# Second mixer: who scales the wide attention rows, and how the values are turned

## The chip, the core and the metric

The kernel runs on one core of one Trainium2 chip. The metric is device time in microseconds (us); each figure without another name is the median of several executions. TensorE (PE) does the matrix products, VectorE (DVE) and ScalarE (ACT) the work on vectors, GpSimd (POOL) and SyncE (SP) issue most of the transfers.

## What is computed

Two layers over 512 tokens of width 1024, in float32. The change lies in the mixer of the second layer: a band attention with 12 heads of 64 columns, whose keys and values are projected from the output of the first layer, beside an attention over 256 memory tokens. Cut to what matters:

```python
ks_, vs_ = jnp.split(rmsnorm(x, kv_norm_g) @ w_kv, 2, axis=-1)      # shared keys and values
...
q, q_mem = jnp.split(h @ b_w_in, [B_WIDTH], axis=-1)
s = jnp.einsum('bqhd,bkhd->bhqk', qc, kc).astype(jnp.float32) * scale + bias
s = jnp.where(valid, s, -jnp.inf)                                   # own chunk and 8 chunks before
p = jax.nn.softmax(s, axis=-1).astype(vc.dtype)
out = jnp.einsum('bhqk,bkhd->bqhd', p, vc)
x = x + jnp.concatenate([mix_out, mem_out], axis=-1) @ w_out
```

## The kernel before

Activations lie transposed: 128 features on the partitions, 512 tokens along the row. Each float32 operand of a product is split in two float32r parts, the high one by a cast on ACT and the low one by a subtraction on DVE (`split`, lines 146 to 151, where the work shows as L147 and L148), and `mm3` (lines 201 to 205) makes three matmuls of each product: high by high, high by low, low by high.

The second mixer goes through six pairs of heads, j = 0 to 5. `project_pair(j)` (line 1477) projects one pair's values, keys and queries: three calls of `project` (line 207), each of 8 k-tiles, so 24 matmuls of 512 columns, with its own weight load of 512 KB on SP's queue (line 162) into one of three "wr" tiles. `times_row` multiplies the projection by the norm's row (L1480). The values come out with features on the partitions, but the product with the attention needs tokens there. So PE turns them: four 128x128 transposes into one PSUM bank (L1491), after the keys' projection and before the queries'. Then `split` makes high and low parts of the turned values out of PSUM, half of the tokens at a time (line 1496; in the profile under L147 and L148).

`band_attention(j)` (line 1501) takes the four tiles T of 128 query tokens in turn, two heads each. `softmax(T)`: the scores of n = 128(T+1) columns on PE (L622); on DVE the bias is added and the row minimum taken (L1518); ACT takes the exponential with its row sum (L1522); DVE takes the sum's reciprocal (L1523) and scales the row by it (L1524). `transposed(T)` turns the scaled rows on PE, 128 columns at a time (L1533), and splits them. At the end the values multiply them (L1554, L1555).

The tiles of the tag "t", 128x512, have eight buffers; the values before they are turned, the scaled rows and the queries before their split all live there. The values' parts lie in "fh" and "fl" (in "u" for the last pair).

Order of the work: `weave` (line 234) mixes an attention with the projections that come later, which serve as its filler: after each step of the attention, so many steps of the filler (one step is one k-tile, three matmuls) by a number written by hand for each pair. Outside of sections marked as manually scheduled, which this one is not, a planner takes this as the order of preference, lets each engine's instructions go when its own costs say that they are ready and a buffer is free, and so writes down one order for each engine and each transfer queue. On the chip every engine and queue keeps to its order, and waits at the head of it.

Of the kernel before, what the change touches and what calls it, by code (L numbers as in the profile page):

```python
# [9 lines left out]
F32 = mybir.dt.float32  # L10
F32R = mybir.dt.float32r
I32 = mybir.dt.int32
AF = mybir.ActivationFunctionType
ALU = mybir.AluOpType
AX = mybir.AxisListType

P = 128
D = 1024
S = 512
KT = D // P  # L20
TT = S // P
# [27 lines left out]
UNITS = {PLAIN + i: tuple((i, j) for j in range(*LOADS[i][2:])) for i in range(len(LOADS))}  # L49

H = S // 2
ORDERED = {mybir.EngineType.PE, mybir.EngineType.Activation, mybir.EngineType.DVE}


def f(ap):
    return ap.bitcast(F32)
# [3 lines left out]
def trunk(  # L60
# [18 lines left out]
    nc = tc.nc  # L79
    V, A, G = nc.vector, nc.scalar, nc.gpsimd  # L80
# [12 lines left out]
    dram = ctx.enter_context(tc.tile_pool(name="dram", bufs=1, space=bass.MemoryType.DRAM))  # L93

    def sb(tag, shape, dtype=F32):
        count[0] += 1
        return pool.tile(shape, dtype, tag=tag, name=f"{tag}{count[0]}", bufs=bufs[tag])

    def ps(tag):
        count[0] += 1  # L100
        return psum.tile([P, S], F32, tag=tag, name=f"p{tag}{count[0]}", bufs=pbufs[tag])
# [12 lines left out]
    ident = cpool.tile([P, P], F32, name="ident")  # L114
# [79 lines left out]
    def weights(*args):  # L194
        return parts(load(*args))
# [11 lines left out]
    def project(w, c0, act, tag="mm", parts=None):  # L207


        n = len(act)  # L210
        wh, wl = parts or weights(rows(w, c0, P), n, P)
        o = ps(tag)
        for k in range(n):
            mm3(o, wh[:, k, :], wl[:, k, :], act[k][0], act[k][1], k == 0, k == n - 1)
            yield
        return o
# [167 lines left out]
    for k in range(KT):  # L384
        if k % 2 == 0:
            src = mem[:, k * P : (k + 2) * P].rearrange("(m p) c -> p m c", p=P)
# [53 lines left out]
    norm = Norm()  # L440
# [168 lines left out]
    def head_keys(t):  # L609
        ks = [sb("u", [P, S], F32R) for _ in range(2)]  # L610
        for h, r in enumerate(HEADS):
            A.copy(ks[h][r, :], t[r, :])
            V.tensor_tensor(out=ks[h][HEADS[1 - h], :], in0=t[r, :], in1=f(ks[h])[r, :], op=ALU.subtract)
        return ks
# [32 lines left out]
    def queries(o, row):  # L647

        if row is None:
            return head_queries(o, HD**-0.5)  # L650
        q = sb("t", [P, S])
        V.scalar_tensor_tensor(q, o, HD**-0.5, row, op0=ALU.mult, op1=ALU.mult)
        return head_queries(q)
# [89 lines left out]
    class ChannelMixer:  # L743
# [54 lines left out]
        def block_sums(self):  # L798

            self.sums = []  # L800
            for k in range(KT // 2):
# [6 lines left out]
                for o, x, y in (  # L808
                    (ta[:, :H], b1[:, H:], b1[:, :H]),
                    (ta[:, H:], b2[:, H:], ta[:, :H]),  # L810
                    (tb[:, :H], b2[:, H:], b1[:, H:]),
                    (tb[:, H:], b2[:, :H], ta[:, H:]),
                ):
# [342 lines left out]
    act = acts  # L1156
# [39 lines left out]
    e, u, c, r = (cpool.tile([P, TT, AH], F32, name=f"gate{i}") for i in range(4))  # L1196
# [253 lines left out]
    norm2, kvact, act = Norm(), [], []  # L1450
# [10 lines left out]
    norm = norm2  # L1461
# [15 lines left out]
    def project_pair(j):  # L1477
        def times_row(o):
            t = sb("t", [P, S])
            V.tensor_tensor(out=t, in0=o, in1=norm.row, op=ALU.mult)  # L1480
            return t

        ov = yield from project(w_kv, AW + j * P, kvact)
        t = times_row(ov) if norm.row is not None else None
        o = yield from project(w_kv, j * P, kvact)
        if t is None:
            t = times_row(ov)
        k = head_keys(times_row(o))
        tp = ps("mm")
        for T in range(TT):  # L1490
            nc.tensor.transpose(tp[:, T * P : (T + 1) * P], t[:, T * P : (T + 1) * P], ident)  # L1491
        v = []
        for i in range(2):

            w = sb("u" if j == 5 else ("fh", "fl")[i], [P, S], F32R).rearrange("p (h c) -> p h c", h=4)
            split(w[:, :, :HD], w[:, :, HD:], tp[:, i * MEM : (i + 1) * MEM].rearrange("p (h c) -> p h c", h=4))
            v += [w[:, :2, :], w[:, 2:, :]]
        q = queries((yield from project(b_w_in, j * P, act)), norm.row)
        qkv[j] = q, k, v

    def band_attention(j, q, k, v):
        pts = [sb("pt", [P, 5 * S], F32R) for _ in range(2)]
        biases = []
        for h in range(2):
            rep = reps[2 * j + h]
            biases.append(sb("bias", [P, S]))
            src = bass.AP(tensor=rep.tensor, offset=rep.offset + P - 1, ap=[[RW - 1, P], [1, S]])
            tc.keep_in_program_order(G.dma_start(biases[h], src))
        es = {}

        def softmax(T):
            n = (T + 1) * P
            ss = [ps("sc")[:, :n] for _ in range(2)]
            scores(ss, q, slice(T * P, n), k, slice(0, n))
            for h in range(2):
                e = sb("t", [P, S])[:, :n]
                mn, sm = small(1), small(1)
                V.tensor_tensor_reduce(  # L1518
                    out=e, in0=ss[h], in1=biases[h][:, S - n :], scale=-1.0, scalar=BIG,
                    op0=ALU.add, op1=ALU.min, accum_out=mn,  # L1520
                )
                A.activation(e, e, AF.Exp, bias=mn, scale=-1.0, accum_out=sm)  # L1522
                V.reciprocal(sm, sm)  # L1523
                V.tensor_scalar(e, e, sm, None, op0=ALU.mult)  # L1524
                es[T, h] = e
            yield

        def transposed(T):
            n = (T + 1) * P
            for h in range(2):  # L1530
                tp = ps("tr")
                for b in range(T + 1):
                    nc.tensor.transpose(tp[:, b * P : (b + 1) * P], es[T, h][:, b * P : (b + 1) * P], ident)  # L1533
                split(
                    blocks(pts[h], (T + 1) * P, 640, T + 1), blocks(pts[h], 3 * 640 + T * P, -768, T + 1),
                    tp[:, :n].rearrange("p (b t) -> p b t", t=P),
                )
            yield

        yield from softmax(0)  # L1540
        yield from softmax(1)
        yield from transposed(0)
        yield from softmax(2)
        yield from transposed(1)
        yield from softmax(3)
        yield from transposed(2)
        yield from transposed(3)
        outs = []
        for h in range(2):
            o2 = ps("tr")  # L1550
            outs.append(o2)
            for s in range(TT):
                w = v[s][:, h, :]
                nc.tensor.matmul(o2[:, s * P :], w, hi_at(pts[h], s, s, TT - s), start=s == 0, stop=False)  # L1554
                nc.tensor.matmul(o2[:, s * P :], w, lo_at(pts[h], s, s, TT - s), start=False, stop=s == TT - 1)  # L1555
            yield
        mixes[j] = values(outs)
# [32 lines left out]
    for hf in range(2):  # L1590
        G.dma_start(fgb[hf], bass.AP(tensor=final_g.tensor, offset=final_g.offset + hf * S, ap=[[0, P], [1, S]]))
    xt = [[None] * 2 for _ in range(TT)]
    B = 32
    xq = []

    def load_quadrants():
# [51 lines left out]
    n = LAST // 2  # L1648
# [129 lines left out]
```

## Time and profile before

| | |
|---|---|
| median of three runs | 1168.01 us (1167.87 to 1168.32) |
| profiled execution, its own time | 1168.55 us |
| its span, from first to last instruction | 1166.5 us |
| PE busy | 1156.2 us, 99% |
| DVE busy | 1001.8 us, 86% |
| ACT busy | 747.9 us, 64% |
| POOL busy | 151.2 us, 13% |
| the second mixer's attentions, about | 613 to 797 us of the span |
| HBM read and written | 133.09 MB and 40.85 MB |

A matmul is pipelined: its record is longer than the distance to the next one, and records overlap. What one costs PE is read from the distance of the starts. The view that groups instructions gives for each group the busy time (overlaps counted once), the mean duration of one, and the idle time of its engine just before. A window row gives, for one stretch of the span, each engine's busy us with its count of instructions in brackets, the granted clock, the share of the DMA engines and GB/s.

### The profile page before, as it was taken

How to read it: one execution, taken by the hardware profiler on the slowest of the kernel's cores; microseconds unless marked ns; L12 is line 12 of the kernel's file. 1: busy time of each engine (PE TensorE's matmuls, PEld its weight loads, DVE VectorE, ACT ScalarE, POOL GpSimd, SP SyncE). 2: the span in 40 equal slices, each digit the busy share in tenths (PEclk: the TensorE clock that was granted, in tenths of full speed). 3: DMA queues.
4: the chain of work that ended last, by engine and by line, in shares of the span. 5: the costliest groups of instructions: out<-in, count | busy, mean ns of one | idle time of the engine just before them, and what ended most of it. 6: DMA issues, size and time to landing. Idle time of an engine off the chain costs nothing.

```text
span 1166.5 us, 19282 instructions
## 1 busy us (share of the span) xinstructions
PE 1156.2 (99%) x7189; PEld 1033.2 (89%) x7189; DVE 1001.8 (86%) x1781; ACT 747.9 (64%) x1343; POOL 151.2 (13%) x254
## 2 busy tenths in 40 slices
PE   9999999999999999999999999999999999999997
PEld 9988888888999999999888888778899999999986
DVE  6877688779999988888797888898999998889977
ACT  6548677657776655555575667776776665555654
POOL 1211101000122222111021000100010111111100
PEclk9999999999999999999999999999999999999999
DMA  8745325244468878777564322335445767777682
GB/s 282 230 110 134 96 56 153 66 134 140 139 157 182 213 178 195 182 173 162 147 193 133 91 62 63 122 107 157 142 126 143 174 146 180 172 180 174 143 157 78
DMA packets 207855, 171.26 MB, mean 147 GB/s; under 512 B 9256, under 2 KB 182030, under 8 KB 207762
## 3 DMA queue, kind: packets, MB, share of 16 engines
q1 hardware_dynamic: 188018, 123.93, 37.1%
q0 software_dynamic: 19168, 45.06, 19.3%
q8 instruction: 56, 0.92, 0.3%
q10 hardware_dynamic: 576, 1.05, 0.2%
q14 instruction: 37, 0.30, 0.1%
HBM read 133.09 MB, written 40.85 MB: 149 GB/s over the span
## 4 chain that ended last, share of the span: by engine, by line
PE 96%; DVE 2%; ACT 1%; DMA 0%; issue 0%; POOL 0%; POOLq 0%; DVEq 0%
PE pmm L203 19%; PE pmm L204 18%; PE pmm L205 18%; PE ptr L204 6%; PE ptr L203 6%; PE ptr L205 6%; PE psc L203 5%; PE psc L204 5%; PE psc L205 5%; PE psc L622 2%; PE ptr L1533 1%; PE ptr L1554 1%; PE ptr L1555 1%; PE ptr L691 1%; PE pmm L513 0%; PE ptr L705 0%
## 5 line engine op out<-in xcount | busy, mean ns | idle before, releaser
L203 PE MATMUL pmm<-u,wh 128*128 128x256 f32 (+1 forms) x992 | 334.9, 338 | 0.1
L205 PE MATMUL pmm<-u,wl 128*128 128x256 f32 (+1 forms) x992 | 332.1, 335 | 0.0
L204 PE MATMUL pmm<-u,wh 128*128 128x256 f32 (+1 forms) x992 | 331.9, 335 | 0.0
L148 DVE TENSOR_TENSOR wl<-wr,wh 128x1024 fp32r<-128x1024 f32 (+4 forms) x165 | 184.8, 1120 | 56.0 <-ACT wh L147 55.4
L205 PEld LDWEIGHTS pmm<-u,wl 128*128 128x128 f32 x992 | 186.3, 188 | 18.9
L203 PEld LDWEIGHTS pmm<-u,wh 128*128 128x128 f32 x992 | 186.4, 188 | 16.7 <-ACT u L147 0.9
L204 PEld LDWEIGHTS pmm<-u,wh 128*128 128x128 f32 x992 | 186.5, 188 | 16.2 <-DVE u L148 0.5
L147 ACT CAST wh<-wr 128x1024 fp32r<-128x1024 f32 (+4 forms) x165 | 159.6, 970 | 62.5 <-PE pmm L204 30.1
L203 PE MATMUL ptr<-u,wh 128*128 128x512 f32 x272 | 106.5, 392 | 0.0
L204 PE MATMUL ptr<-u,wh 128*128 128x512 f32 x272 | 106.3, 391 | 0.0
L205 PE MATMUL ptr<-u,wl 128*128 128x512 f32 x272 | 105.8, 389 | 0.0
L147 ACT CAST fh<-pt 128x512 fp32r<-128x512 f32 x120 | 74.8, 625 | 34.5 <-DVE pt L1059 33.2
L203 PE MATMUL pmm<-u,fh 128*128 128x256 f32 x320 | 88.8, 278 | 0.0
L205 PE MATMUL pmm<-u,fl 128*128 128x256 f32 x320 | 88.6, 277 | 0.0
L204 PE MATMUL pmm<-u,fh 128*128 128x256 f32 x320 | 88.5, 276 | 0.0
L981 ACT COPY t<-pmm 128x256 f32<-128x256 f32 x120 | 45.0, 375 | 67.3 <-PE pmm L205 67.2
L148 DVE TENSOR_TENSOR fl<-pt,fh 128x512 fp32r<-128x512 f32 x120 | 82.3, 687 | 3.1
L765 DVE SCALAR_TENSOR_TENSOR t<-t,cols,t 128x511 f32<-128x511 f32 x88 | 65.9, 749 | 7.3 <-ACT t L772 5.8
L203 PE MATMUL psc<-u,wh 128*128 128x256 f32 (+1 forms) x208 | 63.2, 304 | 0.0
L205 PE MATMUL psc<-u,wl 128*128 128x256 f32 (+1 forms) x208 | 62.9, 302 | 0.0
L204 PE MATMUL psc<-u,wh 128*128 128x256 f32 (+1 forms) x208 | 62.9, 302 | 0.0
L203 PEld LDWEIGHTS pmm<-u,fh 128*128 128x128 f32 x320 | 60.1, 188 | 2.2 <-ACT t L981 0.7
(359 smaller groups left out, 2642.0 us busy)
## 6 DMA issues: line engine op xcount, KB each, us to landing
wr<-in_ffn_w_up_dram SPq DMA_DIRECT2D x46, 512.0 KB, 8.5
pt<-in_ffn_w_up_dram SPq DMA_DIRECT2D x40, 512.0 KB, 8.3
wr<-in_ffn_w_down_dram SPq DMA_DIRECT2D x32, 512.0 KB, 5.4
wr<-in_a_w_in_dram SPq DMA_DIRECT2D x20, 512.0 KB, 3.8
xspill<-bias POOLq DMA_DIRECT2D x32, 256.0 KB, 7.0
without_row<-bias POOLq DMA_DIRECT2D x24, 256.0 KB, 4.1
wr<-in_w_kv_dram SPq DMA_DIRECT2D x12, 512.0 KB, 4.0
without_row<-t POOLq DMA_DIRECT2D x24, 256.0 KB, 4.1
```

Source lines behind the costliest of these rows:

```text
L147: high = A.copy(hi, src) if on_act else V.tensor_copy(hi, src)
L148: low = V.tensor_tensor(out=lo, in0=src, in1=f(hi), op=ALU.subtract)
L203: nc.tensor.matmul(o, lh, rh, start=first, stop=False, skip_group_check=more)
L204: nc.tensor.matmul(o, lh, rl, start=False, stop=False, skip_group_check=more)
L205: nc.tensor.matmul(o, ll, rh, start=False, stop=last, skip_group_check=more)
L622: nc.tensor.matmul(o, a, b, start=first and i == 0, stop=i == 1)
L691: nc.tensor.transpose(tp[:, a, i, :], es[T2, h][:, i, a * P : (a + 1) * P], ident)
L765: V.scalar_tensor_tensor(acc[:, n:], src[:, : S - n], self.fw[:, c * FT + j : c * FT + j + 1], acc[:, n:], op0=ALU.mult, op1=ALU.add,)
L981: A.copy(o, r[:, :H])
L1533: nc.tensor.transpose(tp[:, b * P : (b + 1) * P], es[T, h][:, b * P : (b + 1) * P], ident)
L1554: nc.tensor.matmul(o2[:, s * P :], w, hi_at(pts[h], s, s, TT - s), start=s == 0, stop=False)
L1555: nc.tensor.matmul(o2[:, s * P :], w, lo_at(pts[h], s, s, TT - s), start=False, stop=s == TT - 1)
```

## The change

Two things are changed in the second mixer.

The scaling of the rows by the reciprocal of their sum stays on DVE for T = 0 and 1 (128 and 256 columns) and goes to ACT for T = 2 and 3 (384 and 512 columns).

The values no longer turn on PE. Once multiplied by the norm's row they are written to DRAM from POOL's queue, 256 KB for each pair, with the rows in another order (partition 32a + i goes to row 4i + a). After the queries' projection in program order, four reads on SP's queue fetch them, each into 32 partitions of a new "t" tile: 16 pieces of 32 tokens (128 bytes) for each partition. One block transpose on DVE then turns all 32x32 blocks of the tile into a second "t" tile, which holds the tokens on the partitions, and the split reads that tile in SBUF in place of the PSUM bank. So the split of the values, too, now comes after the queries' projection.

```diff
+B = 32
...
         o = yield from project(w_kv, j * P, kvact)
         if t is None:
             t = times_row(ov)
+        vt = dram.tile([P, S], F32, name=f"values{j}")
+        rows4 = bass.AP(tensor=vt.tensor, offset=vt.offset, ap=[[S, 4], [4 * S, B], [1, S]])
+        G.dma_start(rows4, t)
         k = head_keys(times_row(o))
-        tp = ps("mm")
-        for T in range(TT):
-            nc.tensor.transpose(tp[:, T * P : (T + 1) * P], t[:, T * P : (T + 1) * P], ident)
+        q = queries((yield from project(b_w_in, j * P, act)), norm.row)
+        r, tp = sb("t", [P, S]), sb("t", [P, S])
+        for b in range(4):
+            block = vt[:, b * B :]
+            src = bass.AP(tensor=block.tensor, offset=block.offset, ap=[[4 * S, B], [P, 16], [1, B]])
+            nc.sync.dma_start(r[b * B : (b + 1) * B].rearrange("p (n c) -> p n c", c=B), src)
+        V.transpose(
+            tp.rearrange("p (T a c) -> p a T c", T=TT, a=4), r.rearrange("p (a T c) -> p a T c", T=TT, a=4)
+        )
         v = []
...
-        q = queries((yield from project(b_w_in, j * P, act)), norm.row)
         qkv[j] = q, k, v
...
                 V.reciprocal(sm, sm)
-                V.tensor_scalar(e, e, sm, None, op0=ALU.mult)
+                if T < 2:
+                    V.tensor_scalar(e, e, sm, None, op0=ALU.mult)
+                else:
+                    A.activation(e, e, AF.Copy, scale=sm)
                 es[T, h] = e
```

More of the change, by code (lines that the diff above doesn't have):

```diff
@@ L1592, in trunk @@
     xt = [[None] * 2 for _ in range(TT)]
-    B = 32
     xq = []
```

## The prediction, made before the result was known

> **What bounds the kernel now.** I read the page first, for the engine that fills the span and for the chain that ended last.
>
> ```profile
> span 1166.5 us, 19282 instructions
> PE 1156.2 (99%) x7189; PEld 1033.2 (89%) x7189; DVE 1001.8 (86%) x1781; ACT 747.9 (64%) x1343; POOL 151.2 (13%) x254
> PE 96%; DVE 2%; ACT 1%; DMA 0%; issue 0%; POOL 0%; POOLq 0%; DVEq 0%
> ```
>
> TensorE is busy for 99% of the span, and 96% of the chain runs through it. But records of matmuls overlap, so 99% shows only that PE always had something in flight. Next the window view, for the stretch in which all edited lines run, and for its tightest part.
>
> ```profile
> 613.00:797.00 184.00, 182.87 (x943) 150.68 (x942) 157.01 (x392) 126.19 (x292) 13.11 (x25) 1.00 0.32 96
> 740.00:760.00 20.00, 19.28 (x100) 15.24 (x99) 19.09 (x51) 15.05 (x41) 3.12 (x6) 1.00 0.23 75
> ```
>
> In these 184 us PE lacks work for 184.00 - 182.87 = 1.13 us in all. VectorE is busy 157.01 us (85%), ScalarE 126.19 us (69%), and the DMA engines are used to a third. From 740 to 760 VectorE is full (19.09 of 20), and there lie 0.72 us of PE's 1.13 idle. So the time of this stage is PE's work, with a little lost to VectorE: an edit gains what it takes from PE's queue, plus at most some of these waits.
>
> **What the four transposes cost PE.** This is read from distances of starts in the timeline, not from durations.
>
> ```profile
> L1491 PE MATMUL pmm<-ident,t x24: 270/272/273, 619.6 to 744.6; 128*128 128x128 f32 x24
> ...
> 619.12 0.39 PE L204 MATMUL pmm<-u,wh 128*128 128x512 f32 x1
> 619.35 0.39 PE L205 MATMUL pmm<-u,wl 128*128 128x512 f32 x1
> 619.58 0.60 PE L1491 MATMUL pmm<-ident,t 128*128 128x128 f32 x4
> 619.93 0.48 PE L203 MATMUL pmm<-u,wh 128*128 128x512 f32 x1
> 620.25 0.40 PE L204 MATMUL pmm<-u,wh 128*128 128x512 f32 x1
> ```
>
> A 512-column matmul starts 0.23 us after the one before (619.12 to 619.35). From L205 at 619.35 to L204 at 620.25 there are two such steps, which alone take 0.46 us, and the four transposes: 0.90 - 0.46 = 0.44 us for the four, the slow step behind them (619.93 to 620.25) included. There are 24, in six groups: 6 x 0.44 = 2.64 us. They all lie where PE is the bound, so I take them whole off the path.
>
> The Trainium skill, "TensorE: Matmul & The Clock Gate", section "Part 4: PE-mode transpose", gives about 275 ns for a 128x128 transpose in a kernel. The 270 to 273 ns of L1491 agree with it as the duration of one. As the cost of each it would make the gain 24 x 0.272 = 6.5 us; the four starts at 619.58, all issued by 619.93, speak against that.
>
> **The scaling of rows.** Rows by form, over the stage:
>
> ```profile
> L1522 ACT ACTIVATE t<-t,s 128x512 f32<-128x512 f32 x12 | 8.7, 724 | 3.3 <-DVE s L1518 3.3
> L1522 ACT ACTIVATE t<-t,s 128x384 f32<-128x384 f32 x12 | 7.4, 615 | 3.6 <-DVE s L1518 3.6
> L1523 DVE RECIPROCAL s<-s 128x1 f32<-128x1 f32 x48 | 7.4, 160 | 3.8 <-ACT t L1522 3.3
> L1524 DVE TENSOR_SCALAR t<-t,s 128x512 f32<-128x512 f32 x12 | 5.8, 481 | 0.1
> L1524 DVE TENSOR_SCALAR t<-t,s 128x384 f32<-128x384 f32 x12 | 5.2, 432 | 0.1
> L1611 DVE STREAM_TRANSPOSE u<-pt 128x512 f32<-128x512 f32 x8 | 8.2, 1067 | 0.0
> ```
>
> VectorE loses 12 x 0.481 + 12 x 0.432 = 11.0 us. ScalarE gets 24 activations; the exponential on the same tiles is the nearest row, so 12 x 0.724 + 12 x 0.615 = 16.1 us, and ScalarE goes from 126.2 to 142.3 us of 184, 77%. Neither engine is the bound on average, so the work itself costs nothing beside PE. What it costs is latency: one scaled row comes 0.724 - 0.481 = 0.24 us later (0.18 at 384 columns), plus a handover from VectorE's reciprocal to ScalarE, for which the row of L1523 is nearest, a handover the other way: 3.8 us over 48, 0.08 us each. So 0.26 to 0.32 us a row, and 24 rows make 7 us. Most of it lies beside filler on PE; if ScalarE is behind with its casts it is more, and where VectorE's queue held the row up it is less than nothing. I take zero for the sum and keep both ends. The new wait: ScalarE stands at each scale until the reciprocal is there, and behind it stand the casts that feed PE its split weights and turned rows.
>
> **The new way of the values.** VectorE gets six block transposes. L1611, the only such instruction in the trace, took 1.067 us for the same shape on a strided read; a plain pass over 128x512, L1524, took 0.481. I take the first: 6 x 1.07 = 6.4 us at most, 2.9 at least. With the scales gone VectorE comes to about 157.0 - 11.0 + 6.4 = 152.4 us. The split changes its source from PSUM to SBUF:
>
> ```profile
> L147 ACT CAST u<-pmm 128x256 fp32r<-128x256 f32 x2 | 0.7, 372 | 0.7 <-DVE u L148 0.7
> L147 ACT CAST u<-wr 128x256 fp32r<-128x256 f32 x2 | 0.7, 404 | 0.0
> ```
>
> That is 12 x 0.03 = 0.4 us more on ScalarE, beside other work. The transfers, by the nearest issues:
>
> ```profile
> xspill<-bias POOLq DMA_DIRECT2D x32, 256.0 KB, 7.0
> xspill<-fh POOLq DMA_DIRECT2D x16, 256.0 KB, 2.7
> wr<-in_w_kv_dram SPq DMA_DIRECT2D x12, 512.0 KB, 4.0
> pt<-xspill SPq DMA_DIRECT2D x8, 256.0 KB, 8.2
> L1603 SPq DMA_DIRECT2D pt<-xspill x8: 346/858/1706, 1122.4 to 1128.9; - x8
> L1508 POOL DMA_DIRECT2D bias<-rep x12: 546/547/771, 611.0 to 742.9; - x12
> ```
>
> The write: 0.55 us of issue on POOL (L1508), where bias loads and the zero fills of the query parts stand behind it, and 2.7 to 7.0 us to land. POOL is busy for 13.11 us of the stage's 184; I take nothing for it. The four reads: L1603 is like them, also 32 partitions by 16 pieces, of 512 bytes in place of 128. Each took 0.86 us of SP in the median, so four are 3.4 us (1.4 to 6.8), and 8.2 us to land. Chain: 0.6 + 7.0 + 3.4 + 8.2 + 1.1, and under 2 for the splits, about 22 us at the most. Who needs it, and what stands behind the reads on SP:
>
> ```profile
> SPq L162 <- DVE wl L148: 68.8, 9, 12.2
> ...
> 616.53 5.71 SPq L162 DMA_DIRECT2D wr<-in_w_kv_dram  x2
> ...
> 632.04 1.03 ACT L147 CAST wh<-wr 128x1024 fp32r<-128x1024 f32 x1
> ...
> 670.84 0.42 PE ptr L1554
> ```
>
> The first pair's values turn at 619.6 and first multiply at 670.84, 51 us later, against a chain of 22: hidden. Behind the reads on SP stand the next weight loads. One of them is issued at 616.53, lands after 4.0 us and is cast at 632.04, the third cast on because there are three buffers: 11.5 us to spare, against 3.4 us of issue and a wait for the write's landing. SP stood waiting for such buffers 68.8 us in nine waits, so it has the time. Nothing for the sum. The "t" tiles: two more are held from the reads to the splits, while four scaled rows, the queries and the next values take six of eight. It just fits; a shortage would show as VectorE waiting at L1518.
>
> **The sum.** 1168.55 (the profiled execution, 0.54 above the median 1168.01) - 2.64 = 1165.91 us, so on the median **1165.4**. A measurement of this kernel can tell 0.2% from no change, 2.3 us: below 1165.67 is faster, above 1170.35 slower. The forecast lies just beyond that line.
>
> **Rivals.**
>
> *VectorE's relief counts too.* For it speak these pieces of the chain of waits, and the two rows of the timeline behind them:
>
> ```profile
> 748.91 0.38 ACT u L147
> ...
> 750.73 0.42 DVE u L148
> 751.15 0.47 DVE t L642
> ...
> 753.18 0.51 PE psc L622 x2
> ...
> 640.82 0.48 PE L203 MATMUL pmm<-u,wh 128*128 128x512 f32 x1
> 641.41 0.79 PE L1533 MATMUL ptr<-ident,t 128*128 128x128 f32 x5
> ```
>
> At 748.9 to 751.2 the last pair's value split stands on the chain that ends in PE's wait, and it moves later. At 640.82 a matmul is followed only after 0.59 us, 0.36 too late, though no idle is recorded. If 1.0 to 2.0 us of such waits go: 1163.4 to 1164.4. Against it: the block transposes bring VectorE 6.4 us back.
>
> *ScalarE's latency gives the gain back.* From 740 to 760 ScalarE is at 15.05 of 20 already. If a fifth to a half of the 7 us shows on PE: 1166.8 to 1168.9, no change to be told.
>
> *The block transposes hold VectorE up* (the other side). The planner places each on VectorE where it thinks that the reads have landed; if they land later, VectorE stands, and behind it stand L1518, whose PSUM bank the next scores need, and the subtractions of the weights. PE has about a step or two of filler ready, 0.68 us each by three steps of 0.23. It decides from about 1 us of lateness: 2.5 us late in each of six pairs costs 6 x 1.5 = 9 us, 1174.4; at the line of 1170.35 it takes 6 x 0.83 = 5.0 us. Against it: the order leaves a whole projection between write and reads. The Trainium skill, "DMA: Bandwidth & Descriptors", "Specifications", wants 512 bytes and more for full rate and names a read-modify-write below it, which would make the 128-byte pieces late; no run shown so far has such reads.
>
> *Each transpose costs its duration.* 1168.0 - 6.5 = 1161.5.
>
> **How the numbers follow.** The forecast gets 0.48, with a spread of 0.9 either way (waits that come and go with a new order): 0.29 below the line, 0.19 above. Relief 0.20, all faster. Latency 0.17, all the same. VectorE held up 0.12, slower. Full duration 0.03, faster. Together: faster 0.52, same 0.36, slower 0.12. The range leaves out the last two cases and the edges: 1163.4 to 1169.0.
>
> **What would show it.** Right: no L1491; the projection's matmuls follow at 0.23 us across the place where it stood; the stretch from 613 to 797 is some 2.6 us shorter; 24 activations of about 0.6 to 0.7 us; the reads landed well before VectorE's transposes, with no wait in front of these; L1554 not later than PE comes to it. Wrong: PE waiting for scaled rows (a Copy on ScalarE named as releaser), VectorE idle in front of the block transposes or of L1518, casts of weights waiting for their load, or the stage as long as before though the 24 transposes are gone.

## The result, and the profile after

The changed kernel takes **1179.32 us** (median of 5, 1178.58 to 1180.47) against 1168.17 us of the kernel before in the same session (1167.87 to 1168.58): a ratio of 1.0097, 95% interval 1.0082 to 1.0112. It is 11.15 us slower; 1165.4 us was forecast. First its page, span, engines and chain:

```profile
span 1177.3 us, 19289 instructions
PE 1158.3 (98%) x7165; PEld 1029.9 (87%) x7165; DVE 995.4 (85%) x1763; ACT 761.4 (65%) x1367; POOL 155.6 (13%) x260
PE 92%; ACT 4%; DVE 3%; issue 0%; DMA 0%; POOL 0%; ACTq 0%; DVEq 0%; POOLq 0%
```

The 24 transposes are gone (7165 matmuls, 7189 before), VectorE has less to do and ScalarE more, as forecast. But the chain runs through PE for 92% only, where it was 96%. The window view of the kernel after (PE, PEld, DVE, ACT, POOL busy, clock, DMA share, GB/s) shows where PE lacks work, and one row of the kernel before stands against it:

```profile
613.00:797.00 184.00, 174.45 (x866) 139.69 (x864) 142.22 (x342) 130.06 (x291) 20.44 (x36) 1.00 0.41 110
740.00:760.00 20.00, 17.80 (x90) 13.49 (x89) 19.21 (x39) 15.22 (x36) 5.07 (x9) 1.00 0.54 154
780.00:800.00 20.00, 15.43 (x83) 11.49 (x83) 17.73 (x49) 14.97 (x41) 0.00 (x0) 1.00 0.35 109
```

```profile
780.00:800.00 20.00, 20.00 (x108) 16.36 (x107) 16.52 (x49) 13.28 (x33) 0.00 (x0) 1.00 0.22 64
```

In the stretch of the attentions PE stands for 184.00 - 174.45 = 9.55 us, against 1.13 before. To split the loss I added up PE's steps: what each distance between two starts exceeds the undisturbed step of its width (0.228 us for 512 columns, 0.117 for 256), where it does so by more than 0.1 us. That gives 15.5 us before and 28.9 after, 13.4 more; the undisturbed steps themselves sum to 1149.1 and 1146.4, 2.7 less. 13.4 - 2.7 = 10.7, and the spans differ by 10.8. So the gain is there, and five times as much is lost. Of the 13.4 lie 3.2 in 680 to 720, 2.3 in 740 to 760 and 6.2 in 780 to 800.

The new instructions themselves are no dearer than forecast, but for the write's issue on GpSimd (0.73 us and not 0.55). By line, with least, median and greatest ns, first and last start:

```profile
L1499 DVE STREAM_TRANSPOSE t<-t x6: 701/704/712, 633.4 to 769.7; 128x512 f32<-128x512 f32 x6
L1498 SPq DMA_DIRECT2D t<-values x24: 544/625/817, 628.5 to 763.9; - x24
L1491 POOL DMA_DIRECT2D values<-t x6: 704/726/747, 620.3 to 750.1; - x6
L1536 ACT ACTIVATE t<-t,s x24: 599/664/727, 641.2 to 807.0; 128x384 f32<-128x384 f32 x12, 128x512 f32<-128x512 f32 x12
```

The first sign of trouble is at the first scores. The kernel before, then the kernel after, by their timelines:

```profile
628.90 0.64 PE L622 MATMUL psc<-u,u 128*128 128x128 f32 x4
...
629.27 0.29 DVE L1518 CUSTOM_DVE_ANT_0 t<-psc,bias 128x128 f32<-128x128 f32 x1 [0.17 <-PE psc L622]
```

```profile
628.36 0.64 PE L623 MATMUL psc<-u,u 128*128 128x128 f32 x4
...
632.26 1.23 DVE L149 TENSOR_TENSOR wl<-wr,wh 128x1024 fp32r<-128x1024 f32 x1 [3.70 <-ACT wh L148]
633.40 0.70 DVE L1499 STREAM_TRANSPOSE t<-t 128x512 f32<-128x512 f32 x1
634.03 0.25 DVE L1527 CUSTOM_DVE_ANT_0 t<-psc,bias 128x128 f32<-128x128 f32 x1
```

Before, VectorE takes the scores at once. After, they are ready 0.5 us earlier, but in VectorE's order a weight subtraction and the block transpose stand ahead of them (VectorE waits 3.70 us for the first), and they are taken at 634.03. PE does not stand here: it runs filler. What slips is the attention. First product of the first pair's rows with its values, and the last pair's, before (L1554) and after (L1566):

```profile
643.76 0.39 PE L1554 MATMUL ptr<-pt,fh 128*128 128x512 f32 x1
...
L1554 PE MATMUL ptr<-pt,u x8: 220/306/459, 796.9 to 799.3; 128*128 128x512 f32 x2, 128*128 128x384 f32 x2, 128*128 128x256 f32 x2, 128*128 128x128 f32 x2
```

```profile
L1566 PE MATMUL ptr<-pt,fh x20: 336/368/503, 650.2 to 784.5; 128*128 128x512 f32 x10, 128*128 128x384 f32 x10
L1566 PE MATMUL ptr<-pt,u x8: 220/308/496, 808.2 to 811.0; 128*128 128x512 f32 x2, 128*128 128x384 f32 x2, 128*128 128x256 f32 x2, 128*128 128x128 f32 x2
```

The first is 650.2 - 643.8 = 6.4 us late, the last 11.3 us. Up to 700 PE fills the time with projections taken ahead; after that these run short, and the attention's own waits show.

### The profile page after: what moved, and what is told of

It reads as the page before. It is cut to its first block, busy times and chain, and to the rows that moved or that the text cites. A ratio compares the mean times of both kernels' runs of the same rounds, so it can differ in the third digit from the quotient of the medians.

```text
span 1177.3 us, 19289 instructions
## 1 busy us (share of the span) xinstructions
PE 1158.3 (98%) x7165; PEld 1029.9 (87%) x7165; DVE 995.4 (85%) x1763; ACT 761.4 (65%) x1367; POOL 155.6 (13%) x260
## 4 chain that ended last, share of the span: by engine, by line
PE 92%; ACT 4%; DVE 3%; issue 0%; DMA 0%; POOL 0%; ACTq 0%; DVEq 0%; POOLq 0%
PE pmm L204 18%; PE pmm L205 18%; PE pmm L206 18%; PE ptr L205 6%; PE ptr L204 6%; PE ptr L206 6%; PE psc L204 5%; PE psc L205 5%; PE psc L206 5%; PE psc L623 2%; PE ptr L1545 1%; ACT wh L148 1%; DVE wl L149 0%; DVE pt L149 0%; ACT u L607 0%
## 5 line engine op out<-in xcount | busy, mean ns | idle before, releaser
L149 DVE TENSOR_TENSOR u<-t,u 128x512 fp32r<-128x512 f32 (+1 forms) x80 | 56.5, 711 | 8.8 <-ACT u L148 8.3
```

The lines of the kernel that those rows point to most:

```text
L149: low = V.tensor_tensor(out=lo, in0=src, in1=f(hi), op=ALU.subtract)
```

## The experiments

The theories at the start: **A**, the read and the turned tile share the tag "t" with the softmax rows, and in the written order the rows come behind them; **B**, "t" has too few buffers; **C**, the reads land late and VectorE stands at the block transpose; **D**, ScalarE's scaling is the price. Each run has its kernel before beside it (1168.2 to 1168.4 us).

### The two halves of the change

`e1_scale_only`: the kernel before with

```diff
-                V.tensor_scalar(e, e, sm, None, op0=ALU.mult)
+                if T < 2:
+                    V.tensor_scalar(e, e, sm, None, op0=ALU.mult)
+                else:
+                    A.activation(e, e, AF.Copy, scale=sm)
```

> The kernel before, with only the scaling of the rows of 384 and 512 columns moved to ScalarE; the values turn on TensorE as before. Theory A (the new tiles of the values hold up the softmax, below at the third kernel): ScalarE's later rows cost little, so the time is that of before within 2 us, 1166 to 1170 us. Theory D (the scaling on ScalarE is what slowed the kernel): most of the 11 us are here, 1175 us or more.

`e2_values_only`: the changed kernel with that edit undone.

> The changed kernel with all rows scaled on VectorE again; only the way of the values is new. Theories A, B and C: most of the loss of 11 us is here, 1175 to 1181 us. Theory D: about 1165.5 us, the time before less the 2.6 us of the transposes.

Measured: scaling alone 1179.52 us, ratio 1.0096 (1.0081 to 1.0111); values alone 1172.27, 1.0034 (1.0021 to 1.0047). The halves lose 11.1 and 3.9 us, the whole 11.15: they do not add, and 1172.27 lies in neither range that was expected. With the values' new way in place, the scaling on ScalarE is worth 1179.32 - 1172.27 = 7.05 us, so neither half alone explains the whole. By the sum over PE's steps, the scaling alone loses 1.4 us more in the attentions (613 to 797); 10.5 us are lost between 800 and 830, where the kernel before and the changed one lose under 1. Windows and waits of PE there, in the scaling-alone kernel:

```profile
811.00:817.00 6.00, 1.26 (x4) 0.80 (x4) 6.00 (x10) 6.00 (x10) 2.29 (x5) 0.76 0.60 221
817.00:820.00 3.00, 1.10 (x3) 0.41 (x2) 3.00 (x5) 0.04 (x1) 0.00 (x0) 0.50 0.00 0
820.00:823.00 3.00, 3.00 (x8) 2.33 (x8) 1.81 (x2) 0.00 (x0) 0.00 (x0) 0.50 0.69 206
```

This is behind the last band, where the feed-forward's first projections begin. Two rows of that kernel's timeline, ScalarE's and PE's:

```profile
815.39 1.03 ACT L147 CAST wh<-wr 128x1024 fp32r<-128x1024 f32 x1
...
816.47 0.80 PE L203 MATMUL pmm<-u,wh 128*128 128x512 f32 x1 [4.74 <-DVE rb L298]
```

PE stands 4.74 us, and a little later 1.90 more, and runs on at half clock. The releaser named, the norm's sum on VectorE, is only the last event by the profile: PE starts right when ScalarE has cast this strip's weights (815.39 + 1.03 = 816.42), which it does behind the norm's activations. In the order written for PE, the kernel before has the 24 matmuls of the first strip together here and then the beginnings, two matmuls each, of the second and third. The scaling-alone kernel has 2 of the first, 2 of the second, 2 of the third, and only then the other 22 of the first: the 22 stand behind the third strip's late weights. So the 10.5 us may be a matter of that order (call it D2) and not of ScalarE's time.

### Which tag, or how many buffers

`e3_own_tag`, and `e4_ten_t`:

```diff
-    sizes = {"u": (50, S), ..., "t": (8, S), ...}
+    sizes = {"u": (50, S), ..., "t": (6, S), "tv": (2, S), ...}
...
-        r, tp = sb("t", [P, S]), sb("t", [P, S])
+        r, tp = sb("tv", [P, S]), sb("tv", [P, S])
```

```diff
-    sizes = {"u": (50, S), ..., "t": (8, S), ...}
+    sizes = {"u": (48, S), ..., "t": (10, S), ...}
```

> The changed kernel, but the two new tiles of the values have a tag of their own with two buffers, and the tag t has six instead of eight, so the memory is the same. Theory A (buffers of one tag are handed out in program order, so the softmax rows, which come later in the program, get none until the block transpose has been given its own; VectorE's scores then stand behind the transfers): the scores are taken up as quickly as before, the waits go, and the time is 1164 to 1168 us. Theory B (eight t buffers are too few for the two more tiles): six are fewer still, so 1179 us or more. Theory C (VectorE stands at the block transpose because the reads land late): nothing changes, 1177 to 1181 us.

> The changed kernel with ten buffers of tag t and 48 of tag u instead of 8 and 50. Theory A: more buffers do not change the order in which they are handed out, so the time stays at 1178 to 1181 us. Theory B (too few buffers): the waits go, 1164 to 1168 us. Theory C: 1177 to 1181 us.

Measured: own tag 1173.26 us (1171.45 to 1175.16), ratio 1.0042 (1.0027 to 1.0057); ten buffers 1180.1, 1.0097 (1.008 to 1.0114). With as many buffers in all, the own tag gives 6 us back, though not the 1164 to 1168 that A expected; two buffers more in the shared tag give nothing. B falls. C does not hold for the changed kernel: in its trace each transpose started with 31 ns of idle time before it at most.

Most of what the own-tag kernel still loses is in one place: 4.4 us by PE's steps between 625 and 640. Its waits of PE from 600 to 680, then its window from 630 to 640:

```profile
PE ptr L1545 <- DVE t L1534: 2.7, 2, 1.8
```

```profile
630.00:640.00 10.00, 7.27 (x30) 5.57 (x29) 7.15 (x27) 5.17 (x16) 2.85 (x5) 0.83 0.60 135
```

PE stands for the first pair's rows. In GpSimd's timeline of the changed kernel, against the kernel before, I saw a reason:

```profile
610.99 1.10 POOL L1508 DMA_DIRECT2D bias<-rep  x2
```

```profile
620.25 0.75 POOL L1491 DMA_DIRECT2D values<-t  x1 [10.39 <-PE pmm L206]
...
622.09 1.14 POOL L1517 DMA_DIRECT2D bias<-rep  x2
```

The write of the values waits 10.39 us at the head of GpSimd's queue, and the bias loads behind it are issued at 622.09 and not at 610.99. Call this theory **E**.

### The write on another queue

`e7_own_tag_sp`: the own-tag kernel with

```diff
-        G.dma_start(rows4, t)
+        nc.sync.dma_start(rows4, t)
```

`e8_own_tag_sp_dve`: the same with all rows scaled on VectorE. `e10_write_sp`: the changed kernel with that line alone.

> The changed kernel with the read and turned tile in a tag of their own (as in the own-tag run, 1173.3 us) and the values' write issued by SyncE and not by GpSimd. Theory E: what the own-tag run still loses, 4.4 us between 625 and 640, comes from the first pair's two bias loads, which stand behind the write on GpSimd's queue (issued 622 where they were issued 611 before). With the write elsewhere they are issued at about 611 again, TensorE's stand there and the half clock behind it go, and the time is 1167 to 1169.5 us. Rival: the first pair's scores stand for another reason (ScalarE's scaling or the turned tile), and the time stays at 1172 to 1174 us.

> As the run before in this list, with every row scaled on VectorE as in the kernel before: the values' new path alone, without the shared tag and without the bias loads behind its write. By theory A with E nothing is left of the change but the 24 transposes taken from TensorE: 1168.2 less about 2.6, so 1165 to 1167 us, faster than the kernel before. Rival: the path through memory costs more than these two things: 1168 us or over.

> The changed kernel with nothing altered but that SyncE issues the values' write, so that the bias loads no longer stand behind it; the read and the turned tile stay in the softmax rows' tag. If the two causes stand in one chain of waits (the scores' turn comes behind the block transpose in the tag's order, and the bias is there by then), nothing is gained: 1178 to 1181 us. If they add, the 5.6 us that the own-tag kernel gained from the same edit are gained here too: 1173 to 1175 us.

Measured: 1167.69 us, ratio 0.9996 (0.9986 to 1.0005); 1168.67, 1.0016 (0.9991 to 1.0041); 1178.97, 1.0091 (1.0077 to 1.0105). Beside the own tag the queue is worth 1173.3 - 1167.7 = 5.6 us; with the shared tag nothing, since there the rows come late anyway. VectorE's scaling was expected at 1165 to 1167 and missed that: by the intervals it can't be told from ScalarE's.

E gave the right time for the wrong reason. VectorE's timeline of the own-tag kernel, then of this one, at the first pair:

```profile
628.37 0.29 DVE L1527 CUSTOM_DVE_ANT_0 t<-psc,bias 128x128 f32<-128x128 f32 x1 [0.17 <-PE psc L623]
...
631.82 0.71 DVE L1499 STREAM_TRANSPOSE tv<-tv 128x512 f32<-128x512 f32 x1 [3.15 <-DMA tv<-values]
632.50 0.27 DVE L1527 CUSTOM_DVE_ANT_0 t<-psc,bias 128x128 f32<-128x128 f32 x1
```

```profile
628.64 0.71 DVE L1499 STREAM_TRANSPOSE tv<-tv 128x512 f32<-128x512 f32 x1 [0.18 <-DMA tv<-values]
629.32 0.27 DVE L1527 CUSTOM_DVE_ANT_0 t<-psc,bias 128x128 f32<-128x128 f32 x1
```

The first row has its bias at 628.37, so biases are not what is late. VectorE stands 3.15 us at the block transpose for the reads, and the second row is queued behind it. That is theory C, and the slower rival of the prediction, after all: not in the changed kernel, but in the one with its own tag. The reads are late because the write is. Own tag with the write on GpSimd: the write's issues by line with the least, median and greatest time to landing, then the first pair's write and reads in the timeline:

```profile
L1491 POOL DMA_DIRECT2D values<-t x6: 704/721/747, 620.0 to 744.4; - x6
...
DMA to landing us min/median/max: 6.5/7.1/7.9
...
619.95 0.75 POOL L1491 DMA_DIRECT2D values<-t  x1 [10.45 <-PE pmm L206]
...
627.25 2.67 SPq L1498 DMA_DIRECT2D tv<-values  x4
```

With the write on SyncE the trace has no landing time for it. But SyncE waits for it in front of the reads in all six pairs, as the row of its waits shows, so the start of the reads tells when the write has landed:

```profile
618.10 0.64 SPq L1491 DMA_DIRECT2D values<-t  x1
624.03 2.65 SPq L1498 DMA_DIRECT2D tv<-values  x4
...
SPq L1498 <- DMA values<-t: 31.2, 6, 5.4
```

From issue to the start of the reads it is 5.9 us here, and 5.8 to 6.0 in all six pairs, where GpSimd's writes took 6.5 to 7.9 to land, the first one 7.3. The first write is also issued 1.85 us sooner. Together the reads start 3.2 us sooner (627.25 to 624.03), which is VectorE's stand of 3.15 us. (No run moved the bias loads alone, so this rests on these rows.)

And SyncE's timeline shows what the shared tag does. The second pair's write and its reads, in the changed kernel (the write on POOL), then in this one:

```profile
638.44 0.73 POOL L1491 DMA_DIRECT2D values<-t  x1 [15.21 <-DVE t L1534]
...
649.43 0.37 SPq L163 DMA_DIRECT2D wr<-in_b_w_in_dram  x1
650.29 2.58 SPq L1498 DMA_DIRECT2D t<-values  x4
```

```profile
632.16 0.56 SPq L1491 DMA_DIRECT2D values<-t  x1
638.02 2.82 SPq L1498 DMA_DIRECT2D tv<-values  x4
```

With an own tag the reads are issued 5.9 us after the write, as soon as it has landed. In the shared tag they are issued 11.9 us after it, though that write lands after 7.2: in the order written for SyncE they stand behind a weight load (L163), itself issued only at 649.43. Reads stand right behind a load in five of the six pairs, and the changed kernel's row of waits has one wait for the write in place of six:

```profile
SPq L1498 <- DMA values<-t: 6.3, 1, 6.3
```

The write itself is issued 6.3 us later, too. So the second block transpose comes at 658.45 and not at 645.41, and there, too, the next pair's first rows come right behind it (659.09); behind the own-tag kernel's second transpose there is none.

### One tile alone in the shared tag, and another shared tag

`e17_read_own` and `e18_turned_own` are the 1167.7 us kernel with one of the two tiles back in "t" (7 buffers, and 1 for the other):

```diff
-        r, tp = sb("tv", [P, S]), sb("tv", [P, S])
+        r, tp = sb("tv", [P, S]), sb("t", [P, S])     # e18_turned_own: sb("t", ...), sb("tv", ...)
```

> The own-tag kernel with the write on SyncE (1167.7 us), with only the tile that the reads fill in a tag of its own (one buffer) and the turned tile back among the rows' tag (seven buffers). Its queued order has the even scores in every pair and the memory's scores as in the kernel before. If the read tile is what moved the order, by holding a rows' buffer from an early place in program order until the reads land: 1167 to 1170 us. If the turned tile moved it: 1174 to 1180 us.

> The mirror of the run before in this list: only the turned tile has a tag of its own, the tile that the reads fill is back among the rows' tag. Its queued order has the memory's scores of the fifth pair in one lump of 11 behind a first one, as the changed kernel has. If the read tile is what moved the order: 1173 to 1179 us. If the turned tile did: 1167 to 1170 us.

Measured: 1169.27 us, ratio 1.0008 (0.9999 to 1.0018), and 1169.21, 1.0007 (0.9998 to 1.0017). I expected one of them to be the culprit. Neither is: alone each costs some 1.5 us, together 11.3 (1178.97 with the write on SyncE). The traces fit a chain through both. With the read tile in "t" (`e18_turned_own`), the reads are issued 12 to 15 us after the write from the second pair on, most of them behind weight loads in SyncE's order and one after a wait that ends with a row's scaling, as this row of its waits shows. The transposes come late (633.2 to 763.5), but no row's first step stands right behind them:

```profile
SPq L1498 <- DVE t L1534: 6.9, 1, 6.9
```

With the turned tile in "t" (`e17_read_own`), the reads are issued 6 to 7 us after the write and the transposes come early (629.4 to 757.1), so that rows behind them lose little. Only with both there are the transposes late and the rows right behind them, in five of the six pairs.

That chain is not the whole price. `e2_values_only`, with both tiles in "t" and every row scaled on VectorE, has transposes nearly as late (633.7 to 764.3) and rows right behind five of them, and loses only 3.9 us. No run shows why ScalarE's scaling makes 11 of it.

`e15_u_tag_sp` takes both tiles from the tag "u" (50 buffers), write on SyncE; `e16_u_tag_sp_t3` in addition scales only the rows of 512 columns on ScalarE. Against `e10_write_sp`:

```diff
-        r, tp = sb("t", [P, S]), sb("t", [P, S])
+        r, tp = sb("u", [P, S]), sb("u", [P, S])
...
-                if T < 2:
+                if T < 3:                # e16_u_tag_sp_t3 only
```

> The changed kernel with the read and the turned tile taken from the tag of the activations' parts (u, 50 buffers) in place of the rows' tag, and the values' write issued by SyncE. All six rows' buffers are left to the softmax, the queued order of scores is the even one in the first four pairs and the matmuls behind the last band stand together. If queued order is what decides, what is left is the gain of the transposes, up to 2.5 us: 1165.5 to 1168 us. Rival: the way through memory or ScalarE's scaling has a price of its own, as in the run with all rows on ScalarE (3.6 us): 1169 to 1172 us.

> As the run before in this list, with only the rows of 512 columns scaled on ScalarE. It has less work on ScalarE, but its queued order behind the last band is the broken one (2, 2, 2 and 22). Order theory: TensorE stands behind the last band and runs on at half clock, some 8 to 11 us slower than the run before: 1174 to 1179 us. Rival, ScalarE's work is the price: as fast as the run before or faster.

Measured: 1178.68 us, ratio 1.0091 (1.0076 to 1.0106), and 1187.52, 1.0165 (1.015 to 1.018). The first expectation failed. In PE's order the rows alternate with the filler as they should, but the reads are issued 14 to 33 us after the write from the second pair on, and 3.2 us are lost at 715, behind a cast that waited for its weights, and 6.4 between 780 and 800:

```profile
715.41 1.05 ACT L148 CAST wh<-wr 128x1024 fp32r<-128x1024 f32 x1 [3.33 <-DMA wr<-in_w_kv_dram]
```

Its written order for PE has 100 matmuls of filler between the fourth pair's products and the next scores, where the own-tag order has 59: "u" holds the scores' operands. So out of "t" was not enough; of the tags tried, only the one that nothing else uses was free of the loss. That the 100 matmuls are how the tag "u" came to its 6.4 us is read from the written order and was not tested.

### The order behind the last band

`e5_scale_pinned` and `e6_before_pinned` tried to mend that order by holding the weight splits of the out-projection's last strips, just ahead of it, in program order, in the scaling-alone kernel and the kernel before:

```diff
-                o = self.o[j] if j in self.o else run(project(self.w, j * P, self.mixes))
+                if j in self.o:
+                    o = self.o[j]
+                else:
+                    w = parts(load(rows(self.w, j * P, P), KT, P), pinned=True)
+                    o = run(project(self.w, j * P, self.mixes, parts=w))
```

> The kernel before with the ScalarE scaling alone, and the weight splits of the out-projection's last two strips held in program order. Theory D2: the 10.5 us that the scaling alone lost lay wholly in the order in which matmuls were queued behind the last band (24 matmuls of the first strip no longer together), because TensorE then stood 4.7 us and 1.9 us and ran on at half its clock. With the splits held in order the 24 stand together again: no stand of over 2 us and a granted clock of 1.00 in 805 to 830, and a time of 1168 to 1170.5 us. Rival D: ScalarE's scaling itself makes the attention's rows late by about 10 us: the time stays at 1178 to 1180 us whatever stands at the end.

> Control: the kernel before with the splits of the out-projection's last two strips held in program order and nothing else. If holding them has no price of its own, 1167.5 to 1169 us. If it costs or gains by itself, the scaling's run with the same hold is to be compared with this one and not with the kernel before.

Measured: 1222.53 us, ratio 1.0467 (1.0449 to 1.0484), and 1217.2, 1.0418 (1.0402 to 1.0433). The control shows that the hold itself costs 49 us (PE waits 33.6 us in six pieces for pinned casts, 17.4 of it between 200 and 300, in the first layer, whose out-projection runs through the same lines), so the pair decides nothing. Three others cross order and work. `e9_all_rows_act` scales all 48 rows on ScalarE, `e13_act_first_five` those of 384 and 512 columns in the first five pairs only, `e14_act_last_pair` in the last pair only; each is the kernel before with its condition changed:

```diff
-                V.tensor_scalar(e, e, sm, None, op0=ALU.mult)
+                if T < 2:                # e9: T < 0; e13: T < 2 or j == 5; e14: T < 2 or j < 5
```

> The kernel before with every one of the 48 attention rows scaled on ScalarE (the scaling-alone run, 1179.5 us, had 24 of them there). Its order of matmuls behind the last band is that of the kernel before (24 matmuls of the first strip together), where the scaling-alone run's was 2, 2, 2 and 22. Theory D2: the scaling has no price of its own and the 10.5 us of the scaling-alone run came from that order: twice the scaling on ScalarE costs nothing, 1167 to 1169.5 us, with a granted clock of 1.00 between 800 and 830. Rival D: ScalarE's time or the rows' lateness is the price, so twice as much of it costs at least as much: 1179 us or over.

> The kernel before with the rows of 384 and 512 columns scaled on ScalarE in the first five pairs alone; in the last pair every row is scaled on VectorE. Its queued order behind the last band is broken (2, 2, 2 and 22 matmuls), as in the scaling-alone run. Order theory: TensorE stands behind the last band and its clock falls, 1177 to 1181 us. Rival, ScalarE's work in the last band delays the weight cast: none is there, 1167.5 to 1170.5 us.

> The kernel before with the rows of 384 and 512 columns scaled on ScalarE in the last pair alone. Its queued order behind the last band is that of the kernel before (24 matmuls together). Order theory: 1167.5 to 1170 us. Rival, ScalarE's work in the last band delays the weight cast: 1175 to 1181 us.

Measured: all rows 1171.8 us, ratio 1.003 (1.0018 to 1.0041); first five pairs 1179.71, 1.0097 (1.0082 to 1.0112); last pair 1168.21, 1.0001 (0.9991 to 1.0011). With no scaling on ScalarE in the last band but the broken order behind it, the whole 11 us are lost; with the scaling there and the order whole, nothing. That bears D2 out, though no run changed that order and nothing else. Windows of `e14_act_last_pair`, then `e13_act_first_five`:

```profile
811.00:817.00 6.00, 6.00 (x28) 4.79 (x27) 6.00 (x10) 4.55 (x7) 1.08 (x2) 1.00 0.65 220
```

```profile
811.00:817.00 6.00, 1.97 (x5) 0.80 (x4) 6.00 (x10) 5.40 (x9) 1.98 (x5) 0.74 0.49 178
```

`e16_u_tag_sp_t3`, above, is a fourth: less work on ScalarE than `e15_u_tag_sp`, the broken order, 8.8 us slower, the difference that the order theory expected. The expectation for all rows, 1167 to 1169.5, was missed by some 2 us, so 48 rows on ScalarE do cost something with that order whole, and one more run says the same.

`e12_own_sp_all_act`: the 1167.7 us kernel with all rows on ScalarE.

```diff
-                if T < 2:
+                if T < 0:
```

> The best kernel so far (own tag for the read and the turned tile, write issued by SyncE, 1167.7 us) with all 48 rows scaled on ScalarE. Its queued order of scores and out-projection matmuls is the even one of the kernel before in all of the first four pairs (four scores, three others, four scores), where that kernel's is cut up from the second pair on. If the queued order is what decides, the 1.6 us that it still loses in waits between 640 and 760 shrink: 1165.5 to 1167.5 us, faster than the kernel before. Rival: ScalarE's scaling makes rows late, and it is slower than that kernel: 1168 to 1170 us.

Measured: 1171.61 us, ratio 1.0028 (1.0018 to 1.0038), 3.9 us slower than that kernel. By PE's steps 4.1 more are lost, 1.9 of them between 640 and 680, where PE waits for a scaled row:

```profile
PE ptr L1545 <- ACT t L1536: 1.3, 1, 1.3
```

In all, PE waits 1.7 us for scaled rows here and 0.2 us in `e9_all_rows_act`. Whether the rest of the 3.9 and 3.6 us is the rows' lateness or again the order is not shown.

### What the transposes were worth

`e11_no_turn`: the kernel before without the 24 transposes, values not turned.

```diff
-        tp = ps("mm")
-        for T in range(TT):
-            nc.tensor.transpose(tp[:, T * P : (T + 1) * P], t[:, T * P : (T + 1) * P], ident)
...
-            split(w[:, :, :HD], w[:, :, HD:], tp[:, i * MEM : ...
+            split(w[:, :, :HD], w[:, :, HD:], t[:, i * MEM : ...
```

> The kernel before without the 24 transposes of the values and with nothing in their place: the values' rows go to the split as they stand, so this part of the computation is left out and the time is that of a kernel that need not turn. It is the most that any other way of turning them can gain. By the prediction's price, 24 by 0.11 us, 2.64 us: 1165.2 to 1166 us. If the kernel before hides some of the transposes behind waits: 1166 to 1168 us.

Measured: 1165.7 us, ratio 0.998 (0.9971 to 0.9989), against 1168.19: 2.5 us. With the order otherwise as it is, no way of turning the values elsewhere can bring more. The best kernel with the whole change, own tag and write on SyncE, has 1167.69 and can't be told from the kernel before.

## Why the prediction was wrong

The mechanisms of the chip were mostly right, and the premise of the sum was wrong: it kept the rest of the order as it stood in the trace. Point by point.

- **The four transposes**: right. 2.64 us forecast; 2.5 measured without them, 2.7 by PE's steps. The Trainium skill's 275 ns ("TensorE: Matmul & The Clock Gate", "Part 4: PE-mode transpose", there for bf16) agree with the duration of one here; as a cost they would have given 6.5 us, and 2.5 were measured.
- **The scaling, "I take zero for the sum"**: the durations held (599 to 727 ns, forecast 615 to 724), the zero did not. Alone the edit costs 11 us, and not by the latency that was weighed: it changes the written order behind the last band. In the changed kernel as a whole that order is unbroken (0.7 us lost there), and yet the scaling is worth 7.05 us in it (1179.32 against 1172.27). With the own tag and the write on SyncE it costs nothing (1167.69 against 1168.67 with VectorE). So the zero holds or fails with the order that surrounds it. The forecast latency shows as a wait of PE for a scaled row in three kernels alone: 0.2 and 1.7 us in the two with 48 rows, and 3.3 in `e16_u_tag_sp_t3`.
- **The block transposes**: 0.70 us each and not 1.07, so 4.2 us; the bound taken was too high, to no effect.
- **The chain of transfers**: in all shorter than forecast, though its write is longer. The four reads take 2.6 us of SyncE (3.4) and land in 2.5 to 4.4 (8.2); the write lands in 6.6 to 8.3 on GpSimd's queue (2.7 to 7.0). In the 1167.7 us kernel the first pair takes 618.10 to 629.35, 11.3 us, for write, reads and transpose. The need was misread, though: the product at 670.84 is the second pair's. The first pair's comes at 643.76, 24 us after its values turned and not 51. The chain still fits.
- **"The 't' tiles: it just fits; a shortage would show as VectorE waiting at L1518"**: the step that failed, together with the zero for the scaling. It counted buffers; ten of them change nothing. What counts is who shares the tag: with both new tiles in it, reads stand behind weight loads and rows stand behind the late transposes. Worth 6.1 us with the write on GpSimd (1179.32 to 1173.26), 11.3 with it on SyncE (1178.97 to 1167.69), both with ScalarE's scaling. With VectorE's, shared tag and GpSimd's write together cost 3.6 (1172.27 against 1168.67). Nor does it show as a wait at L1518 (now L1527): it is in the order, and the trace shows other instructions ahead of it.
- **"POOL ... I take nothing for it"**: failed, by another thing than the bias loads named there. With the own tag the first pair's write is issued 1.85 us later from GpSimd than from SyncE and lands 7.3 us after its issue, above the range that was given, and not 5.9, and the reads wait for it. That costs 5.6 us as soon as the shared tag no longer hides it.
- **The slower rival, block transposes that hold VectorE up**: right in its sign and its victim, the rows' first step. In the changed kernel the rows stand behind the transpose by the written order, and the reads have landed. In the own-tag kernel VectorE does stand there, 3.15 us in the first pair (4.1 in three stands); the rival's rule (lateness less 1 us) gives 2.2, and 5.6 were measured: 4.4 of it lie between 625 and 640, where PE stands 2.7 us and then runs at half clock. The 128-byte pieces, of which the Trainium skill warns ("DMA: Bandwidth & Descriptors", "Specifications"), were not what was late: the reads landed in 2.3 to 3.2 us there.

Open is by which rule the order comes to hold the rows back: the runs show that it takes both tiles and a tag with other users, not why. Open is why the loss is 11 us with ScalarE's scaling and 3.9 without. Open, too, is the 2 us between the bound of 1165.7 and the 1167.7 that was reached.

## What to carry to other kernels

Where a planner writes the order, an edit's price is not only its instructions: ask what shares a tag or a queue with each new tile and transfer, give a tile with a long way through memory a tag of its own, and look at how long each queue's transfers took to land before choosing one. An engine that stays busy on filler can hide that the critical work slips; look at when each stage starts, not only at idle time. And before an edit is called dear, try it at twice and half the size, and each half of an edit with and without the other: a cost that falls when the edit grows (11 us for 24 rows, 3.6 for 48) is not the work's own.

## What the runs showed of the chip

A write lands later from one queue than from another, for the same 256 KB and addresses: 6.5 to 7.9 us after its issue from GpSimd's (median 7.1), 5.8 to 6.0 from SyncE's, read from the reads that wait for it. The Trainium skill, "DMA: Bandwidth & Descriptors", "Specifications", gives about 1 and 0.6 us to the first byte on these two ways, the same direction; the traces have some 1.2 us between them to the landing.

PE's clock falls behind a stand and comes back only some us after the work does. In the scaling-alone kernel, behind a stand of 4.74 us, its timeline has 512-column matmuls at twice their usual distance:

```profile
821.04 0.63 PE L205 MATMUL pmm<-u,wl 128*128 128x512 f32 x1
821.47 0.63 PE L203 MATMUL pmm<-u,wh 128*128 128x512 f32 x1
```

0.43 us and not 0.23, at a granted clock of 0.50. With 0.78 granted between 823 and 826 it came back at about 824.3 (x us at half and 3 - x at full speed give 0.78 for x = 1.3), 4.7 us after PE had steady work again at 819.59. Of the 10.5 us lost there 4.74 + 1.90 = 6.6 are waits, and most of the rest is this. The Trainium skill, "TensorE: Matmul & The Clock Gate", section "Why this matters for your kernels", says that a gap of over some 3 us between bursts sends the clock back to half. Here the trace agrees. In the own-tag kernel shorter gaps did it: two stands of 1.79 and 0.94 us, between the starts at 630.85 and 634.76, were enough (0.83 granted over 630 to 640):

```profile
634.76 0.47 PE L1545 MATMUL ptr<-ident,t 128*128 128x128 f32 x1 [0.94 <-DVE t L1534]
...
635.47 0.63 PE L204 MATMUL pmm<-u,wh 128*128 128x512 f32 x1
635.89 0.63 PE L205 MATMUL pmm<-u,wh 128*128 128x512 f32 x1
```
